# A row-wise softmax on one core: the last row of the third tile's load is handed to a second DMA queue, in nine strided pieces

## The chip, the cores and the metric

The kernel runs on one core of one Trainium2 chip. The time is that of the device for one execution, in microseconds (us); the figure given for a kernel is the median of several executions. One of the executions was also recorded by the hardware profiler, and all durations of single instructions and DMA packets come from that one.

## The reference

The input is 16 x 1024 x 512 numbers in float32, that is 16384 rows of 512. Each row is divided by 2 and then put through a softmax:

```
x_scaled = x / 2.0
x_max = max(x_scaled, axis=-1)
exp_x = exp(x_scaled - x_max)
out = exp_x / sum(exp_x, axis=-1)      # float32, same shape
```

So 33.55 MB are read from HBM, 33.55 MB are written, and little is computed on each number.

## The kernel before, in words

The 16384 rows are spread over 128 partitions, 128 rows on each. They are worked through as twelve tiles (the list `PLAN`), numbered 0 to 11. A tile of r rows covers r x 128 consecutive rows of the input; partition p holds rows p*r to p*r + r - 1 of it, so each partition's share is one contiguous run of r x 2048 bytes in HBM, and also in SBUF. The tiles have 3, 7, 15, 15, 15, 15, 15, 15, 15, 7, 3 and 3 rows. They lie in one SBUF tensor, `arena`, of 100 rows a partition. Tiles 0 to 7 fill it; tiles 8 to 11 reuse places of earlier tiles, so their loads wait until the earlier tile has been stored (`behind` lists which).

A tile is worked in chunks of 3 to 5 rows (28 chunks in all), in place. For each chunk VectorE takes the negated maximum of each row (`do_max`, L89), ScalarE makes exp and, with the same instruction, the row's sum (L122), and VectorE takes the reciprocal (L98) and multiplies: in tiles 1, 2 and 3 by one tensor_mul for the chunk (L102), elsewhere by one tensor_scalar for each row (L109). VectorE's order is written out: the maximum of chunk k, then the reciprocal and the multiplication of chunk k - 2 (`LAG`).

Transfers are issued by two engines. ScalarE's queue issues the loads of tiles 0 to 7 (L85): those of tiles 0 and 1 are put ahead of the barrier with which the program begins, the other six behind it, and only then does ScalarE load its table and begin with exp. SyncE's queue issues the twelve stores (L145), each when the tile's last multiplication is done, and between them the loads of tiles 8 to 11 (L152). In the profile ScalarE's queue is q10 and SyncE's is q1. Each load has its own semaphore, `ld[t]`, which a finished DMA raises by 16; the maximum of a chunk waits for 16. GpSimd waits for all the stores at the end.

Of the kernel before, what the change touches and what calls it, by code (L numbers as in the profile page):

```python
# [1 line left out]

# [4 lines left out]

PLAN = [
    ([3], 0), ([4, 3], 3), ([5] * 3, 10), ([5] * 3, 25), ([5] * 3, 40), ([5] * 3, 55),
    ([5] * 3, 70), ([5] * 3, 85), ([5] * 3, 10), ([4, 3], 3), ([3], 0), ([3], 25),
]
ARENA = 100
LAG = 2

FUSED = {1, 2, 3}


@with_exitstack
def kernel(
    ctx: ExitStack,
    tc: tile.TileContext,
    x: bass.AP,
    out: bass.AP,
):
    nc = tc.nc
    fp32 = mybir.dt.float32

    xf = x.flatten_outer_dims()
    of = out.flatten_outer_dims()
    N, D = xf.shape
    P = nc.NUM_PARTITIONS
    n_rows = N // P
    assert sum(sum(c) for c, _ in PLAN) == n_rows

    arena = nc.alloc_sbuf_tensor("arena", (P, ARENA, D), fp32)
    negmax = nc.alloc_sbuf_tensor("negmax", (P, n_rows), fp32)
    sums = nc.alloc_sbuf_tensor("sums", (P, n_rows), fp32)  # L40
    recip = nc.alloc_sbuf_tensor("recip", (P, n_rows), fp32)

    tiles, chunks, base = [], [], 0
    for t, (cs, at) in enumerate(PLAN):
        r = sum(cs)
        tiles.append((base, r, at))
        o = 0
        for c in cs:  # L50
            chunks.append((t, base + o, c, at + o))
            o += c
        base += r
    last_chunk = {c[0]: k for k, c in enumerate(chunks)}

    def dram(ap, t):
        b, r, _ = tiles[t]
        return ap[b * P : (b + r) * P].rearrange("(p r) d -> p r d", r=r)

    def sb(t):  # L60
        _, r, at = tiles[t]
        return arena[:, at : at + r, :]


    behind = {}
    for t, (_, r, at) in enumerate(tiles):
        for u in range(t):
            _, ru, au = tiles[u]
            if at < au + ru and au < at + r:
                behind.setdefault(t, []).append(u)  # L70

    ld = [tc.alloc_semaphore(f"ld{t}") for t in range(len(tiles))]
    awaited = sorted({u for us in behind.values() for u in us})
    st = {t: tc.alloc_semaphore(f"st{t}") for t in awaited}
    s_end = tc.alloc_semaphore("s_end")
    s_max = tc.alloc_semaphore("s_max")
    s_exp = tc.alloc_semaphore("s_exp")
    s_rec = tc.alloc_semaphore("s_rec")
    s_mul = tc.alloc_semaphore("s_mul")

    def issue_loads(begin, end):

        for t in range(begin, end):
            if t not in behind:
                nc.scalar.dma_start(out=sb(t), in_=dram(xf, t)).then_inc(ld[t], 16)  # L85

    def do_max(k):
        t, b, c, a = chunks[k]
        nc.vector.reduce_max(  # L89
            out=negmax[:, b : b + c],  # L90
            in_=arena[:, a : a + c],
            axis=mybir.AxisListType.X,
            negate=True,
        )._wait_ge(ld[t], 16).then_inc(s_max, 1)

    def do_mul(k):
        t, b, c, a = chunks[k]
        nc.vector.reciprocal(  # L98
            out=recip[:, b : b + c], in_=sums[:, b : b + c]
        )._wait_ge(s_exp, k + 1).then_inc(s_rec, 1)  # L100
        if t in FUSED:
            nc.vector.tensor_mul(  # L102
                out=arena[:, a : a + c],
                in0=arena[:, a : a + c],
                in1=recip[:, b : b + c].unsqueeze(2).to_broadcast([P, c, D]),
            )._wait_ge(s_rec, k + 1).then_inc(s_mul, 1)
            return
        for r in range(c):
            ins = nc.vector.tensor_scalar_mul(  # L109
                out=arena[:, a + r],  # L110
                in0=arena[:, a + r],
                scalar1=recip[:, b + r : b + r + 1],
            )
            if r == 0:
                ins._wait_ge(s_rec, k + 1)
        ins.then_inc(s_mul, 1)

    def compute_and_store():

        for k, (t, b, c, a) in enumerate(chunks):  # L120
            for r in range(c):
                ins = nc.scalar.activation(  # L122
                    out=arena[:, a + r],
                    in_=arena[:, a + r],
                    func=mybir.ActivationFunctionType.Exp,
                    bias=negmax[:, b + r : b + r + 1],
                    scale=0.5,
                    accum_out=sums[:, b + r : b + r + 1],
                )
                if r == 0:  # L130
                    ins._wait_ge(s_max, k + 1)
            ins.then_inc(s_exp, 1)


        for k in range(len(chunks) + LAG):
            if k < len(chunks):
                do_max(k)
            if k >= LAG:
                do_mul(k - LAG)


        late = sorted(behind)
        for t in range(len(tiles)):
            nc.sync.wait_ge(s_mul, last_chunk[t] + 1)
            nc.sync.dma_start(out=dram(of, t), in_=sb(t)).then_inc(  # L145
                st[t] if t in awaited else s_end, 16
            )
            while late and max(behind[late[0]]) <= t - 2:
                u = late.pop(0)
                for v in behind[u]:  # L150
                    nc.sync.wait_ge(st[v], 16)
                nc.sync.dma_start(out=sb(u), in_=dram(xf, u)).then_inc(ld[u], 16)  # L152

        for t in awaited:
            nc.gpsimd.wait_ge(st[t], 16)
        nc.gpsimd.wait_ge(s_end, 16 * (len(tiles) - len(awaited)))

    hook = nc.inst_callbacks[-1]  # L160
    nc.remove_inst_callback(hook)
    symbolic = nc._always_lower_symbolic_ap
    nc._always_lower_symbolic_ap = False
    here = str(nc.cur_bb)
    entry = nc.main_func.blocks[0]
    head, jumps = entry.instructions[:-5], entry.instructions[-5:]
    entry.instructions = []
    nc.switch_bb("main", None)
    issue_loads(0, 2)
    first = list(entry.instructions)  # L170
    at = next(k for k, i in enumerate(head) if type(i).__name__ == "InstDrain")
    entry.instructions = head[:at] + first + head[at:]
    issue_loads(2, len(tiles))
    compute_and_store()
    entry.instructions = list(entry.instructions) + jumps
    nc.switch_bb(here, None)
    nc._always_lower_symbolic_ap = symbolic
    nc.push_inst_callback(hook)


# [1 line left out]
_INS = ['x']  # L182
_OUTS = [((16, 1024, 512), 'float32')]


# [23 lines left out]
```

## Time and profile before

| | us |
|---|---|
| time, median of 7 runs | 162.82 (162.43 to 163.12) |
| time of the profiled execution | 162.82 |
| its span, first to last instruction | 161.0 |
| VectorE busy / ScalarE busy | 131.7 / 94.5 |
| first chunk of tile 2 begins on VectorE | 18.13 |
| last store is issued | 143.75 |
| time that the two data queues' packets took, as a share of 16 DMA engines' span | 59.2% + 38.7% |

The profiled execution took as long as the median, and 1.8 us more than its span. The table is read in two halves: the engines' busy times say how much they work, and the last row says how full the 16 DMA engines are. SyncE and ScalarE's issuing of DMAs does not count as busy.

### The profile page before, as it was taken

To read this page: it belongs to the slowest core of one execution; us is meant where nothing else is said; L and a number is where in the kernel's file an instruction comes from. 1 tells how busy PE (TensorE), PEld (TensorE's weight loads), DVE (VectorE), ACT (ScalarE), POOL (GpSimd) and SP (SyncE) were. 2 spreads that over 40 slices of the span, in tenths; PEclk is the share of its full clock that TensorE was granted. 3 is DMA by queue.
4 is the path that set the end of the run, shared out by engine and by line. 5 is a ranking of instruction groups with operands and counts; after the bars stand their busy time and mean duration, and the time that the engine had idled before them with its cause. 6 is when DMAs were issued, how large, how long until landed. Compare 5 with 4: busy or idle time off the path is not lost.

```text
span 161.0 us, 480 instructions
## 1 busy us (share of the span) xinstructions
DVE 131.7 (82%) x155; ACT 94.5 (59%) x257; POOL 0.2 (0%) x4
## 2 busy tenths in 40 slices
DVE  0475499999999999999999999999999999960000
ACT  0739076759547745866669766688666875620000
POOL 0000000000000000000000000000000000000000
DMA  7999999999999999989999999989989999999893
GB/s 254 462 423 458 420 438 409 355 456 388 469 420 412 443 450 404 481 382 468 389 473 389 465 427 422 458 382 433 478 383 423 481 389 465 412 450 443 379 416 128
DMA packets 3459, 67.13 MB, mean 417 GB/s; under 512 B 384, under 2 KB 384, under 8 KB 1152
## 3 DMA queue, kind: packets, MB, share of 16 engines
q1 hardware_dynamic: 2304, 40.90, 59.2%
q10 hardware_dynamic: 1152, 26.21, 38.7%
q14 instruction: 3, 0.02, 0.0%
HBM read 33.55 MB, written 33.55 MB: 417 GB/s over the span
## 4 chain that ended last, share of the span: by engine, by line
DVE 77%; DMA 10%; issue 0%; DVEq 0%
DVE negmax L89 40%; DVE arena L109 22%; DVE arena L102 13%; DMA arena<-in_x_dram 10%; DVE recip L98 2%; DVEq L204 0%
## 5 line engine op out<-in xcount | busy, mean ns | idle before, releaser
L122 ACT ACTIVATE arena<-arena,negmax 128x512 f32<-128x512 f32 x128 | 90.7, 710 | 42.7 <-DVE negmax L89 42.7
L89 DVE TENSOR_REDUCE negmax<-arena 128x5 f32<-128x2560 f32 (+2 forms) x28 | 72.3, 2585 | 11.0 <-DMA arena<-in_x_dram 11.0
L109 DVE TENSOR_SCALAR arena<-arena,recip 128x512 f32<-128x512 f32 x91 | 37.8, 482 | 0.7
L122 ACT ACTIVATION_READ_ACCUMULATOR arena<-arena,negmax 128x1 f32 x128 | 23.9, 187 | 0.0
L102 DVE TENSOR_TENSOR arena<-arena,recip 128x2560 f32<-128x2560 f32 (+2 forms) x8 | 21.0, 2625 | 0.3
L98 DVE RECIPROCAL recip<-sums 128x5 f32<-128x5 f32 (+2 forms) x28 | 4.9, 176 | 0.0
L122 ACT ACT_TABLE_LOAD x1 | 1.3, 1283 | 4.6 <-issue 4.6
L193 POOL MEMSET const-bfloat16-1.0<- 128x1 bf16 x1 | 0.1, 101 | 0.0
L193 POOL MEMSET const-uint8-127<- 128x1 uint8 x1 | 0.1, 101 | 0.0
L193 POOL MEMSET const-float32-0.0<- 128x1 f32 x1 | 0.1, 98 | 0.2 <-issue 0.2
L193 POOL MEMSET const-float32-1.0<- 128x1 f32 x1 | 0.1, 98 | 0.0
## 6 DMA issues: line engine op xcount, KB each, us to landing
out_dram<-arena SPq DMA_DIRECT2D x7, 3840.0 KB, 22.1
arena<-in_x_dram ACTq DMA_DIRECT2D x6, 3840.0 KB, 46.7
arena<-in_x_dram SPq DMA_DIRECT2D x1, 3840.0 KB, 29.9
out_dram<-arena SPq DMA_DIRECT2D x2, 1792.0 KB, 16.6
out_dram<-arena SPq DMA_DIRECT2D x3, 768.0 KB, 15.8
arena<-in_x_dram ACTq DMA_DIRECT2D x1, 1792.0 KB, 8.4
arena<-in_x_dram SPq DMA_DIRECT2D x1, 1792.0 KB, 33.6
arena<-in_x_dram SPq DMA_DIRECT2D x2, 768.0 KB, 34.0
```

The source lines that it names most:

```text
L89: nc.vector.reduce_max(out=negmax[:, b : b + c], in_=arena[:, a : a + c], axis=mybir.AxisListType.X, negate=True,)._wait_ge(ld[t], 16).the ...
L98: nc.vector.reciprocal(out=recip[:, b : b + c], in_=sums[:, b : b + c])._wait_ge(s_exp, k + 1).then_inc(s_rec, 1)
L102: nc.vector.tensor_mul(out=arena[:, a : a + c], in0=arena[:, a : a + c], in1=recip[:, b : b + c].unsqueeze(2).to_broadcast([P, c, D]),)._w ...
L109: ins = nc.vector.tensor_scalar_mul(out=arena[:, a + r], in0=arena[:, a + r], scalar1=recip[:, b + r : b + r + 1],)
L122: ins = nc.scalar.activation(out=arena[:, a + r], in_=arena[:, a + r], func=mybir.ActivationFunctionType.Exp, bias=negmax[:, b + r : b + r ...
L193: nc = _bacc.Bacc("TRN2", target_bir_lowering=False, num_devices=1)
```

## The change

The load of tile 2, the third tile, is cut in two by rows. ScalarE's queue loads the first 14 of its 15 rows, in one DMA at the same place as before, 28 KB a partition where it was 30 KB. The fifteenth row is loaded on SyncE's queue, by nine DMAs that come first on that queue behind the opening barrier. DMA number o (0 to 8) takes partitions o, o + 9, o + 18 and so on: 15 partitions for o = 0 and 1, 14 for the others, 2 KB each. All ten raise the same semaphore, and the three maxima of tile 2 wait for 160. The input that is read, the places in SBUF, and the order of the other instructions on each engine stay as they were.

```diff
+SPREAD = 2
...
         for t in range(begin, end):
-            if t not in behind:
+            if t == SPREAD:
+                r = tiles[t][1] - 1
+                nc.scalar.dma_start(
+                    out=sb(t)[:, :r], in_=dram(xf, t)[:, :r]
+                ).then_inc(ld[t], 16)
+            elif t not in behind:
                 nc.scalar.dma_start(out=sb(t), in_=dram(xf, t)).then_inc(ld[t], 16)
+
+    def issue_spread():
+
+        r = tiles[SPREAD][1] - 1
+        for o in range(9):
+            nc.sync.dma_start(
+                out=sb(SPREAD)[o:P:9, r:], in_=dram(xf, SPREAD)[o:P:9, r:]
+            ).then_inc(ld[SPREAD], 16)
...
-        )._wait_ge(ld[t], 16).then_inc(s_max, 1)
+        )._wait_ge(ld[t], 160 if t == SPREAD else 16).then_inc(s_max, 1)
...
     entry.instructions = head[:at] + first + head[at:]
+    issue_spread()
     issue_loads(2, len(tiles))
     compute_and_store()
```

## The prediction, made before the changed kernel ran

> **What bounds the kernel now.** I read the page first, for how full each engine and the DMA are; then the chain of waits, to see what is late at the start; then busy time by stretches, for the end.
>
> ```profile
> DVE 131.7 (82%) x155; ACT 94.5 (59%) x257; POOL 0.2 (0%) x4
> DMA  7999999999999999989999999989989999999893
> q1 hardware_dynamic: 2304, 40.90, 59.2%
> q10 hardware_dynamic: 1152, 26.21, 38.7%
> ```
>
> VectorE has the longest bar of the engines, and the chain that ended last is nearly all VectorE. But the two data queues together fill 59.2 + 38.7 = 97.9% of 16 DMA engines' span, and the DMA row is full in every slice but the first and the last few. The next rows say what that means (chain; then a group of the timeline; then two DMA issues with KB and us to landing).
>
> ```profile
> 1.42 16.68 DMA arena<-in_x_dram
> 18.13 2.82 DVE negmax L89
> 143.32 0.40 DVE arena L109
> 143.75 0.33 SPq L145 DMA_DIRECT2D out_dram<-arena  x1
> out_dram<-arena SPq DMA_DIRECT2D x1, 3840.0 KB, 21.7
> out_dram<-arena SPq DMA_DIRECT2D x1, 3840.0 KB, 17.6
> ```
>
> The chain has VectorE waiting for loads until 18.13 us and then working without a pause to 143.7. It stops there, yet the span is 161.0: the last 17 us are stores draining. The two issue rows are the stores of tiles 7 and 8, issued at 121.24 and 134.43 us. The first lands at 121.24 + 21.7 = 142.9, so the second waited 8.5 us in the queue behind it; around the other late stores the queue is longer still. VectorE could be several us later and the DMA engines would still not run dry. So DMA throughput sets the end, and in particular the DMA engine that finishes last. This view shows how they finish (window, us, VectorE, ScalarE, GpSimd busy, clock, DMA share, GB/s):
>
> ```profile
> 157.00:157.50 0.50, 0.00 (x0) 0.00 (x0) 0.00 (x0) 1.00 1.00 418
> 157.50:158.00 0.50, 0.00 (x0) 0.00 (x0) 0.00 (x0) 1.00 0.89 369
> 158.00:158.50 0.50, 0.00 (x0) 0.00 (x0) 0.00 (x0) 1.00 0.33 135
> 158.50:159.00 0.50, 0.00 (x0) 0.00 (x0) 0.00 (x0) 1.00 0.21 86
> 159.00:159.50 0.50, 0.00 (x0) 0.00 (x0) 0.00 (x0) 1.00 0.06 25
> ```
>
> The shares add up to 0.5 x (1.00 + 0.89 + 0.33 + 0.21 + 0.06) = 1.25 us beyond 157.0: the mean engine runs dry at 158.25. The trace's packet records, followed from each packet to the one that starts where it ends, give 16 lines of equal bytes with next to no gaps. Twelve end between 157.8 and 158.4, the last four at 158.87, 159.14, 159.20 and 159.62 us; the last landing is at 159.96, and about 1 us of closing barrier follows. Even a perfect balance of the engines would gain only 159.62 - 158.25 = 1.4 us.
>
> **The change, part by part.** Durations are from the profiled execution, which took 162.82 us, exactly the median; its time is its span of 161.0 plus 1.8.
>
> *Bytes.* None added. One packet is one partition's run. The packet records give 234 ns for 6144 bytes, 535 for 14336, 1138 for 30720; so 603 ns for each 16384 bytes more, or 75 for 2048, and a 2048-byte packet should take 234 - 2 x 75 = 84 ns. The semaphore write that ends a DMA on an engine takes 9 ns. Successive packets overlap by about 4 ns.
>
> *Which engine gets them.* The trace shows DMAs over 128 partitions only, equal on all 16 engines: it doesn't say what 14 or 15 partitions do. [...] That makes 15 engines for the first two of the nine, 14 for the rest. Engines 0 to 13 get nine small packets, engine 14 two, engine 15 none, and all lose 8 x 75 = 603 ns from shorter packets on q10. Engines 0 to 13: 9 x (84 + 9) - 603 = +234 ns; less some 4 ns for each of 18 added packets, +0.16 us. Engine 14: 2 x 93 - 603 - 2 x 8 = -0.43 us. Engine 15: -0.60 us. [...]spread evenly over 16, each would get eight packets: 8 x 93 - 603 - 64 = +0.08 us, and nobody is relieved. [...] So what matters is whether the latest engine is 14, 15 or another. The records name no engine. If it is another, the end moves from 159.62 to 159.78. If it is 15, that engine comes to 159.02, but the next, at 159.20, goes to 159.36: a gain of 0.26. If the last two are 15 and 14, the third, at 159.14, goes to 159.30: a gain of 0.32.
>
> [...] By the record of bytes, all are equal; two of the late four owe 0.5 to 0.7 us each to instruction fetches (q14 packets of 309 ns at 75.2 and 99.0 us, each followed by a slowed packet). [...]by chance alone engine 15 or 14 is last in 2 of 16 cases. I give it about a quarter.
>
> *Issuing on SyncE.* Nine DMAs, at 0.33 us (stores, L145) to 0.73 (longest load, L152) each: 3.0 to 6.6 us from 1.4, so done by 8.0. The first thing queued behind them on SyncE is the first store, at 14.37. Cost nothing.
>
> *Issuing on ScalarE.* The same number of DMAs. If the two sequencers hinder each other while they issue, ScalarE's six are later by at most nine issues, 9 x 0.5 = 4.5 us. The rows:
>
> ```profile
> 4.58 1.28 ACT L122 ACT_TABLE_LOAD   x1 [4.58 <-issue]
> 12.86 0.17 DVE L98 RECIPROCAL recip<-sums 128x3 f32<-128x3 f32 x1
> 18.13 2.82 DVE L89 TENSOR_REDUCE negmax<-arena 128x5 f32<-128x2560 f32 x1 [3.78 <-DMA arena<-in_x_dram]
> ```
>
> Then the table load starts at 9.1, ends at 10.4, and the three exp of chunk 0 (2.2 us before) end at 12.6, ahead of the reciprocal. Chunks 1 and 2, 4.9 us of exp, end by 17.5, before tile 2 has landed. Cost nothing.
>
> *Order of the loads.* The small packets now run among those of tiles 0 and 1, which are delayed by at most 256 KB at 420 GB/s, 0.6 us. VectorE idles 3.78 us before 18.13, so tile 1 has that cover. Tile 2 waits for the same bytes as before, plus the 0.16: VectorE starts tile 2 about 0.2 later, or up to 0.5 earlier if its last landing came from the relieved engine. Either is a fraction of the 8.5 us of queued stores. No cost; if that cover were gone, the same 0.2 would appear at the end.
>
> [...] The trace's nearest row is the first load: 768 KB, 4.5 us from issue to landing, of which 8 x 234 ns = 1.9 is data. If each of nine paid the other 2.6 in turn, the row would land at 1.4 + 9 x 2.7 = 26, VectorE would be 8 us late, and the end might just be touched. But the eight loads of ScalarE are issued some 0.5 us apart with the engines filled behind them, so overheads overlap with other DMAs' data. I count the packets alone.
>
> Sum: 162.82 + 0.16 = 162.98, say 163.0. Unknown is the price of a small packet: below, 0 over its bytes (then +0.0); above, what 6144-byte packets cost on q10, mean 284 ns, 50 more than their norm because of the start: 9 x 50 = 0.45 more, so 163.4.
>
> **Rivals.**
> 1. *The latest engine is a relieved one* (15, or 15 and 14). For it: [...]four stand out at the end. Against: the lateness of two is instruction fetch and the rest scattered stalls. Time 162.5.
> 2. *Small packets leave bubbles: slower.* On engines that are full all the time a lost ns is not recovered. At the start the first packets took 638 to 807 ns instead of 234. If a 2 KB packet between larger ones loses even 50 ns, the nine cost 0.45 more, 163.4. It decides against "no change" from (0.33 - 0.16) / 9 = 19 ns a packet on. Against it: steady rows show no such loss at 6144 bytes.
> 3. *The nine gather on one engine*[...]: 128 x 93 ns = 11.9 us on one, less 0.6, against a mean end 1.4 before the last: near 172. [...]
> 4. *The split does nothing:* even spreading, 162.9; it belongs with the forecast.
>
> **How the numbers follow.** A measurement of this kernel can tell about 0.2%, 0.33 us, from no change. Forecast with rival 4: 0.47 (0.36 within, 0.09 slower, 0.02 faster, from run to run differences in which engine is last). Rival 1: 0.27, half of it over 0.33 (0.13 faster, 0.14 within). Rival 2: 0.22 (0.20 slower, 0.02 within). Rival 3: 0.04, slower. Together 0.15 faster, 0.52 within, 0.33 slower. Range: 162.4, below rival 1, to 163.6, above rival 2's 163.4; outside are rival 3 and tails.
>
> **What would show it.** q1 should have 128 more packets of 2048 bytes; the DMA rows stay full; SyncE's nine issues end before 8 us; tile 2 begins on VectorE within 0.5 of 18.13; VectorE still ends some 17 us before the span. If rival 1 holds, the shares after 158.5 shrink and the last landing is before 159.7. If rival 2, all stretches from 2 to 8 us move fewer GB/s and the whole drain is later. Rival 3 shows as a long tail of one engine, a share of 0.06. I am wrong if VectorE is pushed 8 us late, or if the time moves by over 0.6 with the drain's form unchanged.

## The result, and the profile after

The changed kernel took 163.81 us (median of 13 runs, 163.19 to 164.33), the kernel before in the same comparison 162.81. The ratio is 1.0061, with a 95% interval of 1.0044 to 1.0078: slower by 0.6%, or 1.0 us, outside the range that was forecast. The profiled execution took 164.17 us with a span of 162.4, 1.35 us more than the profiled execution before. The comparisons here and below leave out runs over 1.5% above the fastest of the same kernel.

The page first: engines, DMA by slices, the two data queues.

```profile
DVE 131.7 (81%) x155; ACT 94.5 (58%) x257; POOL 0.2 (0%) x4
DMA  7999999999999999999999999999989999999991
q1 hardware_dynamic: 2560, 41.16, 59.5%
q10 hardware_dynamic: 1152, 25.95, 38.0%
```

The work of the engines is the same to 0.1 us and the DMA row is full, as before. q1 has 256 packets more (128 of data, 128 semaphore writes), as the split says. The chain of waits shows the first surprise (start, us, what; `SPq L98` is SyncE issuing one of the nine DMAs):

```profile
7.30 0.76 SPq L98
8.06 0.04 issue
8.11 15.08 DMA arena<-in_x_dram
23.18 0.02 issue
23.21 2.82 DVE negmax L104
```

The chain no longer runs through the 14 rows on ScalarE's queue but through the last of the nine small DMAs. It was issued at 8.11 us and ended 15.08 us later. VectorE began tile 2 at 23.21, where it had been 18.13. Everything that VectorE does later, and so every store but the first, moved by some 5.1 us; the last store is issued at 148.8 us instead of 143.75. The reason is in the DMA queues of the changed kernel between 12 and 18 us (packets; then queue, packets, MB, share of 16 engines):

```profile
DMA packets 181, 2.44 MB, mean 407 GB/s; under 512 B 58, under 2 KB 58, under 8 KB 100
q10 hardware_dynamic: 97, 2.36, 96.5%
q1 hardware_dynamic: 84, 0.09, 4.2%
```

In 6 us q1 started 84 packets and moved 0.09 MB; q10 started 97 and moved 2.36 MB. The engines that had packets of both queues alternated between the queues packet by packet, 2 KB against 28 KB, and the 4-byte semaphore write behind each small packet took a turn of its own (of the 58 packets under 512 bytes, 42 are these; the other 16 end the 14-row load on q10). In the packet records 81 packets of 28 KB start between 10 and 16 us: 36 of them where a 2 KB packet of q1 ends, 34 where a semaphore write of q1 does, and 11 where another 28 KB packet does, on the two engines that had no small packet then. So a small DMA cost an engine two turns, and between two turns passed one packet of 28 or 30 KB, some 1.1 us (28 KB took 1.12 in the mean). The records show the rhythm. One engine, followed from packet to packet, reads: 2 KB of q1 at 10.72 us, 28 KB of q10 at 10.81, a semaphore write of q1 at 11.95, 28 KB of q10 at 11.95, the next 2 KB of q1 at 13.05. So small packets start in groups 2.3 us apart, and the last semaphore write of the nine goes at 22.7.

At the end, the shares of the 16 engines:

```profile
157.00:157.50 0.50, 0.00 (x0) 0.00 (x0) 0.00 (x0) 1.00 1.00 418
157.50:158.00 0.50, 0.00 (x0) 0.00 (x0) 0.00 (x0) 1.00 0.94 393
158.00:158.50 0.50, 0.00 (x0) 0.00 (x0) 0.00 (x0) 1.00 0.68 283
158.50:159.00 0.50, 0.00 (x0) 0.00 (x0) 0.00 (x0) 1.00 0.44 184
159.00:159.50 0.50, 0.00 (x0) 0.00 (x0) 0.00 (x0) 1.00 0.30 123
159.50:160.00 0.50, 0.00 (x0) 0.00 (x0) 0.00 (x0) 1.00 0.15 61
160.00:160.50 0.50, 0.00 (x0) 0.00 (x0) 0.00 (x0) 1.00 0.06 25
160.50:161.00 0.50, 0.00 (x0) 0.00 (x0) 0.00 (x0) 1.00 0.06 25
```

The shares add up to 0.5 x 3.63 = 1.82 us beyond 157.0, so the mean engine is dry at 158.82, against 158.25 before: 0.57 later. The last packet ends at 161.0, against 159.62: 1.4 later. So the loss has two parts of like size: all engines lose some time, and the last one falls further behind the mean (2.2 us in place of 1.4).

Where do they lose it? Here are four microseconds in which SyncE's queue serves the load of tile 10, the one with 6144-byte packets: first the kernel before, then the changed one (window, us, VectorE, ScalarE, GpSimd busy, clock, DMA share, GB/s; a packet counts whole where it starts, so a short window can show a share over 1).

```profile
110.00:114.00 4.00, 4.00 (x5) 2.82 (x9) 0.00 (x0) 1.00 1.07 453
```

```profile
110.00:114.00 4.00, 4.00 (x5) 2.98 (x10) 0.00 (x0) 1.00 1.07 407
```

The engines are just as busy and move 10% less. These GB/s are a coarse sign, though: two kernels of the experiments below, of which only one loses time, move 436 and 434 here. The packets themselves are a better one. In the packet records the 6144-byte packets of this window took 239 ns in the mean before, 292 after. Each engine has eight of them, so that is 8 x 53 = 0.42 us of the 0.57.

### The profile page after: what moved, and what is told of

It reads as the page before. It is cut to its first block, busy times and chain, and to the rows that moved or that the text cites. A ratio compares the mean times of both kernels' runs of the same rounds, so it can differ in the third digit from the quotient of the medians.

```text
span 162.4 us, 489 instructions
## 1 busy us (share of the span) xinstructions
DVE 131.7 (81%) x155; ACT 94.5 (58%) x257; POOL 0.2 (0%) x4
## 3 DMA queue, kind: packets, MB, share of 16 engines
q1 hardware_dynamic: 2560, 41.16, 59.5%
## 4 chain that ended last, share of the span: by engine, by line
DVE 77%; DMA 9%; SPq 4%; issue 1%; DVEq 0%
DVE negmax L104 40%; DVE arena L124 22%; DVE arena L117 13%; DMA arena<-in_x_dram 9%; SPq L98 4%; DVE recip L113 2%; DVEq L220 0%
```

## The experiments

Three reasons stood against one another: the small packets cost DMA time (rival 2 of the prediction), the load is uneven over the engines, or VectorE's late start, which I had costed at nothing, moves the stores to where they do harm.

**The same transfers without the late start.** The nine DMAs get their own semaphore, and only the third chunk of tile 2, which holds the fifteenth row, waits for it.

```diff
-            ).then_inc(ld[SPREAD], 16)
+            ).then_inc(ld_row, 16)
...
+        lands, n = ld[t], 16
+        if t == SPREAD and k == last_chunk[t]:
+            lands, n = ld_row, 144
-        )._wait_ge(ld[t], 160 if t == SPREAD else 16).then_inc(s_max, 1)
+        )._wait_ge(lands, n).then_inc(s_max, 1)
```

> Only the wait differs from the changed kernel: the first two chunks of tile 2 wait for the 14-row DMA alone, the third chunk, whose last row it is, also for the nine. All transfers stay. VectorE should begin tile 2 at about 18.0 us in place of 23.2. If the time was lost because VectorE's late start moved the stores, this comes back to 162.8 to 163.0. If it was lost in the DMA engines (the turns of the small packets, or fourteen engines with more to do), it stays at 163.6 to 163.9.

Measured: 162.81 us, ratio to before 1.0002 (0.9985 to 1.0019). The chain of this kernel:

```profile
1.42 16.98 DMA arena<-in_x_dram
18.40 0.02 issue
18.42 2.82 DVE negmax L108
```

VectorE starts tile 2 at 18.42, and the whole microsecond is back, with every small packet still there. The transfers in themselves cost nothing that this comparison can see (about 0.3 us at most, by its interval).

**The late start without the transfers.** The kernel before, with two extra maxima ahead of tile 2.

```diff
+    unused = nc.alloc_sbuf_tensor("unused", (P, 9), fp32)
...
+        if k == 3:
+            for o, w in ((0, 5), (5, 4)):
+                nc.vector.reduce_max(
+                    out=unused[:, o : o + w],
+                    in_=arena[:, a : a + w],
+                    axis=mybir.AxisListType.X,
+                )._wait_ge(ld[t], 16)
```

> The kernel before, with two extra maxima of 5 and 4 rows (4.9 us) on VectorE ahead of tile 2, whose results are not used; all transfers as before. VectorE begins tile 2's own maxima at about 23.0 us. If the late start alone costs the time: 163.6 to 163.9. If VectorE's 8.5 us of queued stores cover it: 162.6 to 163.0.

Measured: 164.13 us, ratio 1.0086 (1.0056 to 1.0116). The timeline of this kernel:

```profile
18.00 5.01 DVE L92 TENSOR_REDUCE unused<-arena 128x5 f32<-128x2560 f32 x2 [3.81 <-DMA arena<-in_x_dram]
22.93 2.81 DVE L97 TENSOR_REDUCE negmax<-arena 128x5 f32<-128x2560 f32 x1
```

Without a single changed DMA, a start 4.9 us late costs at least as much as the change. Together the two runs settle which part of the change costs the time: the late start. How a late start costs it, they do not say.

**One even DMA, and the nine on one queue.** First, the last row by a single DMA over all 128 partitions on SyncE's queue; second, the nine issued by ScalarE, behind the 14 rows.

```diff
-        for o in range(9):
-            nc.sync.dma_start(
-                out=sb(SPREAD)[o:P:9, r:], in_=dram(xf, SPREAD)[o:P:9, r:]
-            ).then_inc(ld[SPREAD], 16)
+        nc.sync.dma_start(
+            out=sb(SPREAD)[:, r:], in_=dram(xf, SPREAD)[:, r:]
+        ).then_inc(ld[SPREAD], 16)
...
-        )._wait_ge(ld[t], 160 if t == SPREAD else 16).then_inc(s_max, 1)
+        )._wait_ge(ld[t], 32 if t == SPREAD else 16).then_inc(s_max, 1)
```

> The last row of tile 2 by one DMA over all 128 partitions on SyncE's queue, in place of nine: every engine has 8 small packets and one semaphore write, nine turns with the other queue in place of eighteen, and the same load on all 16. The row should land before the 14 rows do, so VectorE begins tile 2 at about 18.0 us. If the eighteen turns or the uneven load or VectorE's late start cost the time: 162.8 to 163.1. If it is the small packets themselves: 163.4 to 163.8.

Measured: 162.53 us, 0.9990 (0.9977 to 1.0003); tile 2 starts at 18.10. A DMA over all 128 partitions has eight packets and one semaphore write for each of 16 engines (in the profile before, 24 such loads and stores make 3072 packets of data and 384 semaphore writes), so by this count an engine took nine turns for the row, and the row was there in time.

```diff
-    issue_spread()
-    issue_loads(2, len(tiles))
+    issue_loads(2, 3)
+    issue_spread()
+    issue_loads(3, len(tiles))
...
-            nc.sync.dma_start(
+            nc.scalar.dma_start(
```

> The same nine DMAs, issued on ScalarE's queue right behind the 14 rows: same packets and same uneven load, but one queue, so no turns. ScalarE issues for some 7 us longer (about 12 us in place of 4.6) and starts exp at about 13 us; tile 2 should land at 18.0 to 18.5. If the turns or VectorE's late start cost the time: 162.8 to 163.1. If it is the uneven load: 163.6 or more.

Measured: 162.42 us, 0.9992 (0.9977 to 1.0007); tile 2 starts at 19.02, half a microsecond later than I had expected. ScalarE loads its table at 12.21, and the first store leaves at 17.3 in place of 14.4, which costs nothing. The same uneven load, with nothing to take turns with, cost nothing. Neither is a gain.

**Which stores may not be late?** The two extra maxima again, ahead of the last chunk of tile 7, of tile 5 and of tile 3 (`k == 20`, `14` and `8` in the diff of the second experiment).

> The kernel before, with the same two extra maxima (4.9 us, results unused), but ahead of the last chunk of tile 7: stores 0 to 6 and the late loads are issued when they were before, stores 7 to 11 about 5 us later. If the late end of VectorE costs the time (queues running low in the drain): 163.6 to 164.2, as with the delay ahead of tile 2. If it is the lateness of the stores before that: 162.4 to 162.9.

Measured: 162.65 us, 1.0001 (0.9984 to 1.0018).

> The same 4.9 us ahead of the last chunk of tile 5: stores 0 to 4 and the loads of tiles 8 to 10 are issued as before, store 5, the load of tile 11 and stores 6 to 11 about 5 us later. If store 6, then issued at 111 us while the 6144-byte packets of tile 10's load run, stalls those packets: 163.2 to 163.8, with the stalls at 110 to 114 us. If the loss comes from the early stores, which leave ScalarE's loads alone for longer and spread the engines: 162.4 to 162.9.

Measured: 162.54 us, 0.9994 (0.9974 to 1.0014). My expectation of harm from store 6 fell.

> The 4.9 us ahead of the last chunk of tile 3: stores 0 to 2 on time, store 3 at about 67, store 4 at 82 and the late loads from 82 us, as with the delay ahead of tile 2. If the loss comes from stores 3 and 4 and the loads behind them: 163.6 to 164.2. If from stores 1 and 2: 162.4 to 162.9.

Measured: 164.01 us, 1.0079 (1.0050 to 1.0108).

In all three the last stores are issued as late as in the second experiment (the last one at 148.5 or 148.6 us). So the queue ahead of the late stores does cover 4.9 us at the end, as the prediction had it. The harm comes from stores 3 and 4 and the loads of tiles 8 to 10 behind them: being late by 4.9 us from there on is enough, being late only from store 5 on does nothing. Which of these stores and loads does it, no run separates.

**Does it grow with the delay?** One extra maximum of 5 rows, run twice; then 2 rows, and 5, 5 and 4 rows.

> The kernel before with one extra maximum of 5 rows (2.7 us) ahead of tile 2. If the loss is proportional to the lateness: 163.2 to 163.5. If it begins only when some cover is used up: 162.4 to 162.9.

Measured: four of the six executions took 167.1 to 167.9 us, the other two 164.32 and 166.40 us; these two give 1.0165 (1.0095 to 1.0236).

> The kernel with 2.7 us of extra maxima ahead of tile 2, once more. In its first run one DMA engine ended 5 us after all others. If that belongs to this lateness: again about 167. If it came from that loading of the program: 162.6 to 163.6.

Measured: 20 of the 22 executions took 167.0 to 168.5 us, the other two 162.62 and 164.16 us; these two give 1.0043 (1.0000 to 1.0087). In the profiles one DMA engine (first run) or five (second) end some 5 us after the others. Why is open; I draw nothing from these runs but that this kernel's time jumps by some 5 us.

> The kernel before with one extra maximum of 2 rows (1.1 us, result unused) ahead of tile 2. If the cost grows with the lateness: 162.8 to 163.0. If it is a matter of phase, anything from 162.4 to 167, and the engines out of step at 68 to 85 us exactly where the time is longer.

Measured: 162.60 us, 1.0009 (1.0000 to 1.0019).

> The same with extra maxima of 5, 5 and 4 rows (7.7 us). If the cost grows with the lateness from the 1.4 us that 4.9 us cost: 164.7 to 165.5. If it is a matter of phase: anything from 162.4 to 167, with more engines out of step at 68 to 85 us where it is longer.

Measured: 163.43 us, 1.0060 (1.0043 to 1.0077): less than 4.9 us of delay cost, where proportion asked for 164.7 or more. And the loss has another form. Two windows of this kernel:

```profile
140.00:145.00 5.00, 4.96 (x11) 3.36 (x10) 0.00 (x0) 1.00 0.55 233
145.00:150.00 5.00, 4.89 (x13) 3.10 (x10) 0.00 (x0) 1.00 1.15 492
```

Here the DMA engines do run dry, between 140 and 145 us: store 7 landed at 142.2, and store 8 was only issued at 142.0. That is the end of the cover that I had read as 8.5 us. Afterwards all 16 engines end within 0.2 us of one another (packets end at 160.07 to 160.23), where the drains of the kernels that are as fast as before spread over 1.2 us or more. The semaphore writes, one for each engine, show where that comes from. While no engine was idle, their lag on one another stayed: the 16 writes of store 7 spread over 1.8 us in the kernel before and 3.1 in the changed one, and those of the last store over 1.8 and 2.9. Here they spread over 1.1 us at store 7 and 0.2 from store 8 on, for which all engines had waited. So the dry stretch makes the mean engine 1.8 us later than before, but the last one only 0.6.

**An earlier start.** Tile 2 in three DMAs of 5 rows, each chunk waiting for its own.

```diff
+            if t == 2:
+                for j in range(3):
+                    nc.scalar.dma_start(
+                        out=sb(t)[:, 5 * j : 5 * j + 5],
+                        in_=dram(xf, t)[:, 5 * j : 5 * j + 5],
+                    ).then_inc(ld_part[j], 16)
...
-        )._wait_ge(ld[t], 16).then_inc(s_max, 1)
+        )._wait_ge(ld_part[k - 3] if t == 2 else ld[t], 16).then_inc(s_max, 1)
```

> Tile 2 loaded on ScalarE's queue as three DMAs of 5 rows over 128 partitions, each with its own semaphore, and each chunk waits for its own. Same bytes, 256 more packets, of 10240 bytes in place of 30720 (about 0.2 us an engine), two more issues on ScalarE. VectorE begins tile 2 at about 14.4 us in place of 18.1, so all later stores are some 3.7 us earlier. If earliness pays as lateness costs: 162.0 to 162.3. If the stores are covered already: 162.5 to 163.0.

Measured: 162.69 us, 1.0003 (0.9987 to 1.0020), with tile 2 started at 14.20. An earlier start is not worth anything, but only stores 1 to 5 were really earlier, by 3.3 to 3.9 us: at 97.10 us VectorE had waited 3.78 us for the load of tile 7, and stores 6 to 11 left 0.6 us later than before. That all later stores would be earlier, as I had expected, was wrong.

**Another order of the late loads.** SyncE issues the loads of tiles 10, 9, 8, 11, each as soon as its place is free, in the changed kernel and in the kernel before.

```diff
-        late = sorted(behind)
+        late = sorted(behind, key=lambda u: max(behind[u]))
```

> The changed kernel, with SyncE's late loads in the order of tiles 10, 9, 8, 11, each as soon as its place is free: tile 10 (6144-byte packets) behind store 2, at about 50 us, while ScalarE's loads still run, in place of about 85. VectorE still begins tile 2 at 23.2. If the loss is the stalls of tile 10's small load packets at 110 to 114 us: 162.8 to 163.2 and no stalls there. If the late stores cost by themselves: 163.6 to 163.9.

Measured: 163.49 us, 1.0060 (1.0041 to 1.0079).

> The kernel before with the same order of late loads. In it tile 10's packets hardly stalled (0.07 us an engine), so 162.4 to 162.8 under each theory; a gain over 0.3 us would say that the order alone helps.

Measured: 163.12 us, 1.0026 (1.0012 to 1.0040).

The stalls of tile 10's packets at 110 to 114 us are gone in both, since those packets run elsewhere; the time is not. So these stalls are where the loss shows itself, not what must be removed. The order alone costs 0.3%, which I had not expected. In that kernel VectorE has waited 2.75 us for the load of tile 8 at 114.14, so stores 7 to 11 leave 2.9 us later; but lateness from store 7 on cost nothing above.

**Eight even DMAs, and the change once more.** Eight DMAs over every eighth partition, in place of nine.

```diff
-        for o in range(9):
+        for o in range(8):
-                out=sb(SPREAD)[o:P:9, r:], in_=dram(xf, SPREAD)[o:P:9, r:]
+                out=sb(SPREAD)[o:P:8, r:], in_=dram(xf, SPREAD)[o:P:8, r:]
...
-        )._wait_ge(ld[t], 160 if t == SPREAD else 16).then_inc(s_max, 1)
+        )._wait_ge(ld[t], 144 if t == SPREAD else 16).then_inc(s_max, 1)
```

> The changed kernel with eight DMAs over every eighth partition (16 partitions each) in place of nine: every engine gets 8 small packets and 8 semaphore writes on SyncE's queue, the load is even. The row should land at about 21 us, so VectorE starts some 3 us late. If uneven load adds to the loss: below the changed kernel's 163.8 by more than the lateness explains, about 162.9. If lateness and phase set it: like the delay of 2.7 us (up to 167) or like the changed kernel.

Measured: 162.67 us, 1.0006 (0.9991 to 1.0022), but three of the 14 executions took 166.7 to 166.9 us, a jump like that of the kernel with 2.7 us of delay. Tile 2 starts at 19.49, 1.4 us late, not 3. Two turns fewer are some 2.2 us by the 1.1 us above, and the small DMAs were also issued sooner, the last one at 5.91 us in place of 8.11. The ratio agrees with the delay of 1.1 us. It doesn't say anything on even load by itself, because the start moved with it.

> The changed kernel once more, for a second profile. 163.5 to 164.1; if loss of step is its cause, 4 to 6 of 16 engines out of step at 68 to 85 us again, against 2 to 3 in the kernels that are as fast as before.

Measured: 164.12 us, 1.0080 (1.0050 to 1.0110), tile 2 started at 22.85. One of the seven executions took 162.69 us, as little as the kernel before, with the same program.

**What the delay does to the DMA engines.** From the packet records I counted, each 20 ns between 68 and 85 us, how many of the 16 engines were in a packet of SyncE's queue and how many were not, and took the smaller number: 0 if all serve the same queue, 8 if they are split in halves. Beside it, the mean of the 6144-byte packets at 110 to 114 us:

| kernel | ratio | engines out of step | 6144-byte packets, ns |
|---|---|---|---|
| before | 1 | 2.5 | 239 |
| late wait / one DMA / ScalarE's queue | 1.0002 / 0.9990 / 0.9992 | 2.9 / 2.2 / 2.1 | 241 / 239 / 238 |
| late from store 7 / from store 5 | 1.0001 / 0.9994 | 2.5 / 2.3 | 243 / 239 |
| early / 1.1 us late / eight | 1.0003 / 1.0009 / 1.0006 | 2.6 / 2.3 / 2.8 | 246 / 236 / 245 |
| changed kernel, two profiles | 1.0061, 1.0080 | 4.7, 3.7 | 292, 304 |
| 4.9 us late (profile of its fastest execution, 163.29 us) | 1.0086 | 6.2 | 269 |
| late from store 3 | 1.0079 | 5.4 | 323 |
| 2.7 us late, two profiles, of executions of 167.85 and 167.40 us | see above | 4.4, 4.3 | 249, 279 |

In the kernel before and the eight that are as fast, at most three engines are out of step. In the three that lose by lateness, 3.7 to 6.2 are (3.7 in the second profile of the changed kernel, where I had expected 4 to 6), and small load packets then take 30 to 85 ns longer. SyncE's issuing of the loads of tiles 8 to 10 divides the kernels in the same way: 0.54, 0.49 and 0.51 us in the kernel before, 1.48, 1.46 and 1.72 in the changed one, and for all of them 0.47 to 0.80 us in the nine kernels against 1.29 to 2.22 in the four profiles of the three. All this fits a matter of phase: whether the engines keep step would depend on where stores 3 and 4 fall against ScalarE's loads. Step and slow issuing were observed together with the loss in each profile; no run forced either by itself, so whether they are its cause or further signs of it is not shown. Nor does the count of engines give the size: with 2.7 us of delay it is 4.4, and most executions lose some 5 us. Outside the pattern are 7.7 us late (1.7 engines; its loss is the dry queue) and the two kernels with the other order of loads (2.1 engines for the changed one and 2.9 for the one before, and slower all the same). Why those lose time stays open.

## Why the prediction was wrong

*What held.* DMA throughput sets the end (the last store is issued 13.6 us before the end of the span, and the two queues fill 59.5 + 38.0 = 97.5% of it), and VectorE's busy time doesn't matter: 4.9 us more of it, ahead of store 5 or of store 7, cost nothing (0.9994 and 1.0001). That the DMAs of 15 partitions use 15 engines and those of 14 use 14 was my assumption; its counts agree with the trace: q1 has 128 more semaphore writes, which is 2 x 15 + 7 x 14, one for each engine used, and from 9 to 16 us two of the 16 engines had no small packet. Which engines they are, no record shows: the numbers 0 to 15 are names, and the quarter given to one of the relieved two being last was my estimate. A 2048-byte packet took 84 ns in the median, as worked out. The price of the packets, +0.16 us, is compatible with the run that keeps all transfers and removes the late start (1.0002, 0.9985 to 1.0019). ScalarE's issuing was covered (its table load began at 4.92 us, where it had been 4.58); SyncE issued for 7.45 us, 0.76 for most of the nine, ended at 8.9 where I had written by 8.0, and had the cover that was named.

*The first step that failed* is "Order of the loads": "VectorE starts tile 2 about 0.2 later" was a wait taken as a sum of bytes. I let the small packets run among those of tiles 0 and 1 by their bytes, 256 KB at 420 GB/s. The queues did not share by bytes. The small packets waited their turn, eighteen turns of up to 1.1 us on an engine, and VectorE started 5.1 us late. I had the number that warns of this, nine data packets and nine semaphore writes for an engine, in the sum, and used it for their cost alone, not for their waiting. The paragraph on the first load's 4.5 us did weigh a landing at 26 us, close to the 23.2 that came, and put it aside, because overheads overlap with other DMAs' data. The engines were indeed busy with other data meanwhile (q10 took 96.5% of them from 12 to 18 us); that did nothing for the transfer that waited, which landed 15.08 us after its last DMA was issued.

*The second step that failed* is the cover: "Either is a fraction of the 8.5 us of queued stores. No cost". At the end the cover is real: lateness from store 5 or 7 on costs nothing, and the queue runs dry only with 7.7 us. But I read it from the last stores alone. The same 5 us from store 3 on cost 0.8% (1.0079), with the last stores issued no later than in the runs that lost nothing. "The DMA engines are full" was taken to mean that order can't matter; full engines took 292 ns for a 6144-byte packet where they had taken 239, and the last of them ended 1.4 us later. The late start, costed at nothing, cost 1.0 us in the changed kernel. Why lateness at stores 3 and 4 has this effect stays open.

*Rival 1* asked for relief of the latest engine. Nothing of it can be seen: the kernels with the same uneven load and a timely start are not faster (1.0002 and 0.9992). *Rival 2* had the sign, and 163.4 at 50 ns a packet, 0.4 us short of the measured time, but for another reason: its bubbles around the 2 KB packets would have shown in the late-wait kernel, which has all these packets. *Rival 3* did not occur: the nine DMAs have 128 packets and 128 semaphore writes, and 14 of the 16 engines took them turn by turn from 9 to 16 us. I had no rival in which VectorE's lateness matters below the cover; that is the one that came.

## What to carry to other kernels

In the changed kernel's trace two queues shared a DMA engine by packets, so a transfer of small packets and many semaphore writes on a second queue arrived late beside one of large packets, few as its bytes were (256 KB, landed at 23.2 us): count the turns, and let only the work that needs such a transfer wait for it (1.0002 in place of 1.0061). One DMA over all partitions took half the turns of nine strided ones, nine for eighteen, and cost nothing (0.9990). And a full DMA row was no cover for late stores in the middle of the program (1.0079 from store 3 on): test the lateness itself, with a few useless instructions, before costing it at zero.

## What was not expected of the hardware

A semaphore write of 4 bytes (9 ns) took a turn between queues like a packet of 30 KB (1138 ns). SyncE needed 0.76 us to issue a DMA of 14 partitions, and 0.33 us for a store of 128. Delays of 1.1, 4.9 and 7.7 us ahead of tile 2 cost 0.1% (the edge of its interval), 0.9% and 0.6%, and one of 2.7 us some 5 us in most executions: the time wasn't monotonic in the delay. No run was faster than the kernel before by more than its interval.
